# Turning attention probabilities with 64-row transposes inside the score bursts of a two-layer encoder

## The chip, the cores and the metric

The kernel runs on one NeuronCore of one Trainium2 chip. The metric is the device time of one execution in microseconds (us), the median of several runs; lower is better. Engines are named as in the profile: PE is TensorE's matmul side, PEld its weight loads, DVE is VectorE, ACT is ScalarE, POOL is GpSimd, SP is SyncE, on whose queue the DMAs are issued.

## The reference

256 tokens of width 1024 go through two layers in float32. Layer 0 (even) has two groups of eight heads side by side: neighbourhood attention with a bias table, and latent attention (MLA). Layer 1 (odd) has 16 heads of 64; each head is a mixture of three dilated windows. Every layer ends with a squared-ReLU MLP.

```python
def odd_mixer(xn, w_in, w_o, cos_f, sin_f):
    hcat = (xn @ w_in).reshape(b, s, DIL_GROUPS, 3, DIL_HEADS, HEAD_DIM)
    q = apply_rope(hcat[:, :, :, 0], cos_f, sin_f)
    k = apply_rope(hcat[:, :, :, 1], cos_f, sin_f)
    v = hcat[:, :, :, 2]
    return dilated_attention(q, k, v) @ w_o
...
for layer in range(DEPTH):
    xn = rms_norm(x, norm_mix[layer])
    x = x + (even_mixer(...) if layer % 2 == 0 else odd_mixer(...))
    x = x + sq_relu_mlp(rms_norm(x, norm_mlp[layer]), mlp_w1[layer], mlp_w2[layer])
return rms_norm(x, norm_final)
```

Every attention is scores = q k, a softmax over the keys, and a sum of the values weighted by the probabilities.

## The kernel before

**Matrix products.** Weights stream from HBM through `load_weight` (DMA into `raw`, SP's queue) and are split by `split` into a high part (ACT, line 176) and a low part (DVE, line 177). `mm3` (lines 180 to 182) and `mm2` (lines 186 and 187) are the large products on PE in 128x128 mode; they are called "gemm" here. A gemm matmul streams 256, 384 or 512 columns.

**Attention on PE.** Three other shapes of the array occur. `two_heads` (line 201) makes the scores of two heads at once: each head has 64 rows of the array, three passes a head. The two smaller window groups of the odd layer (line 880) use 64x64 tiles. The sums of values, `mix` (lines 730, 913, 918), have 64 columns a head. Between scores and sums the probabilities must be turned so that the keys lie on partitions: `turn_probs` (even, line 714) and `turn` (odd, line 898) do this with transposes of 128x128 blocks on PE, in the shape of the gemm, and a copy out of PSUM (lines 716, 900).

**PSUM** has eight banks, four under the tag "w" and four under "acc". `bank(tag)` takes them in turn, and an instruction that writes a bank waits until the readers of its last use are done.

**Even layer.** `attention()` gives a list of 35 side steps that is spread over the gemm steps of `main` by a cost per step. `items` numbers the 16 (kind, query tile, head pair): numbers 0 to 7 are neighbourhood attention, with two query tiles t for each of the four head pairs hp, and 8 to 15 are MLA. `scores(n)` stands at side step 2n+1 (number 0 at step 0), `turn_probs(n-1)` right behind it, and the sums at n = 5 (pairs 0 and 1), 9 (2 and 3), 13, 15 and 17. A bias tile of 256 KB per item comes by DMA into one of two buffers (`load_bias`, line 679); the next load into a buffer waits for the reduction on DVE (line 699) that reads it. After it come the exponentials and the scaling on ACT (lines 704 and 707).

**Odd layer.** The 16 heads are eight units of two heads. Of each unit u, twelve gemm steps make q and k (`qk_steps`, with a swap by DMA for the rotation) and four the values. `weave` spreads the attention of unit u-1 over these 16 steps: a burst (scores by `two_heads`, then line 880, then `mix` of unit u-2) behind the first step, then four single turns with a gemm step or two between them. `mix` of unit 6 stands at the end of unit 7's gemm, the attention of unit 7 and its `mix` in the output product (`out_steps`).

The instruction order on each engine is that of a list scheduler which starts from the program's order and may put a ready instruction ahead of one that its model takes for late.

## Time and profile before

| what | us |
|---|---|
| median of 3 runs (lowest to highest) | 744.56 (744.52 to 745.54) |
| the profiled execution | 744.40 |
| its span, first to last instruction | 742.6 |
| PE busy in the span | 734.6 |
| PEld busy | 645.2 |
| DVE busy | 536.2 |
| ACT busy | 464.2 |

The granted clock of TensorE was 0.999 of full speed. The even attention lies at about 40 to 107 us of the span, the odd layer at about 305 to 562 us. Matmuls are pipelined: a matmul's row shows its latency, so what PE spends on a piece is read from the distance between starts, not from the busy time.

### The profile page before, as it was taken

To read this page: it belongs to the slowest core of one execution; us is meant where nothing else is said; L and a number is where in the kernel's file an instruction comes from. 1 tells how busy PE (TensorE), PEld (TensorE's weight loads), DVE (VectorE), ACT (ScalarE), POOL (GpSimd) and SP (SyncE) were. 2 spreads that over 40 slices of the span, in tenths; PEclk is the share of its full clock that TensorE was granted. 3 is DMA by queue.
4 is the path that set the end of the run, shared out by engine and by line. 5 is a ranking of instruction groups with operands and counts; after the bars stand their busy time and mean duration, and the time that the engine had idled before them with its cause. 6 is when DMAs were issued, how large, how long until landed. Compare 5 with 4: busy or idle time off the path is not lost.

```text
span 742.6 us, 12516 instructions
## 1 busy us (share of the span) xinstructions
PE 734.6 (99%) x4764; PEld 645.2 (87%) x4764; DVE 536.2 (72%) x1108; ACT 464.2 (63%) x1044; POOL 6.0 (1%) x16
## 2 busy tenths in 40 slices
PE   9999999999999999999999999999999999999996
PEld 6998998888888888989899899898998888888885
DVE  6798869666665666898777787787769665665664
ACT  6679967554554556767775866877757544554541
POOL 0100000000000000000000000000000000000000
PEclk9999999999999999999999999999999999999999
DMA  8966334555555444674655555565653545455401
GB/s 286 344 205 222 114 121 163 186 212 180 178 209 185 179 174 150 197 249 154 224 185 183 188 189 179 171 189 192 232 199 126 215 169 209 169 190 193 178 26 56
DMA packets 28107, 136.87 MB, mean 184 GB/s; under 512 B 4496, under 2 KB 7056, under 8 KB 14992
## 3 DMA queue, kind: packets, MB, share of 16 engines
q1 hardware_dynamic: 27760, 135.81, 53.4%
q8 instruction: 37, 0.61, 0.3%
q10 hardware_dynamic: 288, 0.28, 0.1%
q14 instruction: 22, 0.18, 0.1%
HBM read 127.68 MB, written 1.05 MB: 173 GB/s over the span
## 4 chain that ended last, share of the span: by engine, by line
PE 91%; ACT 3%; DMA 2%; issue 1%; DVE 1%; SPq 0%; POOLq 0%; POOL 0%; DVEq 0%; ACTq 0%
PE w L186 16%; PE acc L180 13%; PE acc L181 13%; PE acc L182 13%; PE acc L186 12%; PE w L187 8%; PE acc L187 6%; PE w L898 1%; PE acc L913 1%; PE w L201 1%; DMA raw<-in_w_v 1%; PE w L730 1%; DMA bias<-in_rpb 1%; PE w L714 1%; ACT whi L176 1%
## 5 line engine op out<-in xcount | busy, mean ns | idle before, releaser
L177 DVE TENSOR_TENSOR wlo<-raw,whi 128x512 fp32r<-128x512 f32 (+3 forms) x488 | 302.5, 664 | 63.5 <-ACT whi L176 63.0
L176 ACT CAST whi<-raw 128x512 fp32r<-128x512 f32 (+3 forms) x488 | 263.7, 602 | 82.6 <-issue 71.1
L186 PE MATMUL w<-xT,whi 128*128 128x512 f32 x512 | 179.4, 394 | 0.0
L186 PE MATMUL acc<-xT,whi 128*128 128x512 f32 x384 | 137.3, 401 | 0.0
L187 PE MATMUL w<-xT,wlo 128*128 128x256 f32 x512 | 132.8, 280 | 0.0
L186 PEld LDWEIGHTS w<-xT,whi 128*128 128x128 f32 x512 | 93.6, 187 | 18.3
L187 PEld LDWEIGHTS w<-xT,wlo 128*128 128x128 f32 x512 | 96.1, 188 | 5.5
L187 PE MATMUL acc<-xT,wlo 128*128 128x256 f32 x384 | 99.8, 280 | 0.0
L180 PE MATMUL acc<-whi,h 128*128 128x512 f32 x250 | 98.4, 393 | 0.0
L181 PE MATMUL acc<-wlo,h 128*128 128x512 f32 x250 | 97.8, 391 | 0.0
L182 PE MATMUL acc<-whi,h 128*128 128x512 f32 x250 | 97.4, 390 | 0.0
L186 PEld LDWEIGHTS acc<-xT,whi 128*128 128x128 f32 x384 | 70.0, 188 | 12.7
L193 ACT COPY up<-w 128x256 f32<-128x256 f32 x64 | 23.9, 374 | 88.4 <-PE w L186 88.4
L187 PEld LDWEIGHTS acc<-xT,wlo 128*128 128x128 f32 x384 | 72.2, 188 | 3.7
L194 DVE TENSOR_TENSOR up<-up,w 128x256 f32<-128x256 f32 x64 | 26.8, 419 | 63.0 <-ACT up L193 62.3
L180 PE MATMUL acc<-whi,xT 128*128 128x384 f32 (+2 forms) x160 | 56.6, 354 | 0.1
L181 PE MATMUL acc<-wlo,xT 128*128 128x384 f32 (+2 forms) x160 | 56.1, 351 | 0.3 <-DVE wlo L177 0.2
L182 PEld LDWEIGHTS acc<-whi,h 128*128 128x128 f32 x250 | 46.9, 188 | 10.1
L181 PEld LDWEIGHTS acc<-wlo,h 128*128 128x128 f32 x250 | 47.0, 188 | 9.8
L182 PE MATMUL acc<-whi,xT 128*128 128x384 f32 (+2 forms) x160 | 55.4, 346 | 0.0
L180 PEld LDWEIGHTS acc<-whi,h 128*128 128x128 f32 x250 | 46.9, 188 | 9.1
L181 PEld LDWEIGHTS acc<-wlo,xT 128*128 128x128 f32 x160 | 30.3, 190 | 3.0 <-DVE wlo L177 2.0
(194 smaller groups left out, 1021.3 us busy)
## 6 DMA issues: line engine op xcount, KB each, us to landing
raw<-in_w SPq DMA_DIRECT2D x64, 1024.0 KB, 4.8
raw<-in_w_oqk SPq DMA_DIRECT2D x24, 1024.0 KB, 5.1
raw<-in_w_ov SPq DMA_DIRECT2D x16, 768.0 KB, 4.5
sw<-qk SPq DMA_DIRECT2D x96, 64.0 KB, 2.2
raw<-in_w_qk SPq DMA_DIRECT2D x4, 1024.0 KB, 10.8
raw<-in_w_oe SPq DMA_DIRECT2D x4, 1024.0 KB, 7.1
raw<-in_w_oo SPq DMA_DIRECT2D x4, 1024.0 KB, 5.0
bias<-in_rpb SPq DMA_DIRECT2D x8, 256.0 KB, 5.4
```

The lines of the kernel that those rows point to most:

```text
L176: a = nc.scalar.copy(hi, src).ins
L177: return a, (eng or nc.vector).tensor_tensor(lo, src, hi.bitcast(F32), op=ALU.subtract).ins
L180: nc.tensor.matmul(o, sh, mh, start=first, stop=False)
L181: nc.tensor.matmul(o, sh, ml, start=False, stop=False)
L182: nc.tensor.matmul(o, sl, mh, start=False, stop=last)
L186: both = lambda: nc.tensor.matmul(o, sh, m.rearrange("p v n -> p (v n)"), start=first, stop=last)
L187: low = lambda: nc.tensor.matmul(o[:, 0:T], sl, m[:, 0, :], start=False, stop=False)
L193: nc.scalar.copy(dst, o[:, T:2 * T])
L194: nc.vector.tensor_tensor(dst, dst, o[:, 0:T], op=ALU.add)
L201: nc.tensor.matmul(o[j], qk[pb, 0, a, ts], qk[pb, 1, b, :], start=n == 0, stop=n == 2)
L714: nc.tensor.transpose(pt[:, b * P:(b + 1) * P], pp[:, b // 2, (b % 2) * P:(b % 2 + 1) * P], ident)
L730: nc.tensor.matmul(pvo[64 * j:64 * j + 64, o], v[:, kk, h * 64:(h + 1) * 64], pts[:, 2 * j + kk, :], start=kk == 0, stop=kk == NT - 1)
```

## The change

- **Odd layer, turns.** `turn(u, i)` now takes query tile i for both heads: per head three blocks of 128 keys, each by two transposes of 64 rows (rows 0 to 63 and 64 to 127 of the probabilities, with the matching 64x64 part of the identity). The two halves go to two PSUM banks `pt[0]` and `pt[1]`; two copies put them together in one tile `pts`. 12 transposes a turn in place of 6 in two turns.
- **Odd layer, place.** Both turns of unit u-1 stand in the burst of unit u: `mix(u-2)`, `turn(u-1, 0)`, the `two_heads` scores, `turn(u-1, 1)`, line 880's scores. So the sum of values of a unit comes one burst later, and the value tiles have three buffers. The turns' banks are of the tag "acc" there. The burst stands behind the second gemm step (for unit 0 behind the fourth); the burst of unit 7 stands behind step 13 of unit 7's own gemm. In the output product `last_turn` (`mix` of unit 6, both turns of unit 7) stands behind step 6 and `mix` of unit 7 behind step 9.
- **Even layer.** The two query tiles of a head pair in neighbourhood attention are one burst: `pair_scores(hp)`, 12 matmuls, at side steps 0, 5, 9 and 13. `turn_pair(hp-1)` (16 transposes of 64 rows) stands ahead of it, and ahead of that `mix(hp-2)`. The last pair (items 6 and 7) and MLA keep `turn_probs`. `mix` takes the sums of turned pairs in halves of 64 queries. `load_bias` is called behind the softmax that frees the buffer.

```diff
@@ -679,22 +679,28 @@
                 nc.sync.dma_start(biases[n], a["rpb"][t, hp])
 
         def scores(n):
-            kind, t, hp = items[n]
-            load_bias(n + 2)
-
-            sb = [bank("w")[:, 0:T] for _ in range(2)] if kind == 0 else bank("w").rearrange("p (j n) -> p j n", j=2)
-            s_of = lambda j: sb[j] if kind == 0 else sb[:, j]
-            if kind == 0:
-                two_heads(sb, qk[hp], tok(t))
-            else:
-                for j in range(2):
-                    h = 2 * hp + j
-                    q, k = (halves(mT[n][:, h]) for n in "qk")
-                    mm3(sb[:, j], q[0][:, tok(t)], q[1][:, tok(t)], *k, True, True)
+            hp = items[n][2]
+            o = bank("w").rearrange("p (j n) -> p j n", j=2)
+            for j in range(2):
+                h = 2 * hp + j
+                q, k = (halves(mT[c][:, h]) for c in "qk")
+                mm3(o[:, j], q[0][:, tok(items[n][1])], q[1][:, tok(items[n][1])], *k, True, True)
+            softmax(n, [o[:, 0], o[:, 1]])
+
+        def pair_scores(hp):
+            o = [bank("w") for _ in range(2)]
+            for t in range(NT):
+                two_heads([z[:, t * T:(t + 1) * T] for z in o], qk[hp], tok(t))
+            for t in range(NT):
+                softmax(2 * hp + t, [z[:, t * T:(t + 1) * T] for z in o])
+                load_bias(2 * hp + t + 2)
+
+        def softmax(n, s):
+            kind = items[n][0]
...
+                o = s[j]
...
             pt = bank("w")
             for b in range(4):
                 nc.tensor.transpose(pt[:, b * P:(b + 1) * P], pp[:, b // 2, (b % 2) * P:(b % 2 + 1) * P], ident)
-            turned[n] = scratch([4, P], "pts")
-            nc.any.tensor_copy(out=turned[n], in_=pt.rearrange("p (b n) -> p b n", b=4))
+            pts = scratch([4, P], "pts")
+            nc.any.tensor_copy(out=pts, in_=pt.rearrange("p (b n) -> p b n", b=4))
+            turned[n] = [(slice(0, P), lambda b: pts[:, b, :])]
+
+        def turn_pair(hp):
+
+            pt, pts = [bank("w") for _ in range(2)], [scratch([8, 64], "pts") for _ in range(2)]
+            for t in range(NT):
+                pp = probs.pop(2 * hp + t)
+                for b in range(4):
+                    for r in range(2):
+                        rows, at = slice(64 * r, 64 * r + 64), slice((4 * t + b) * 64, (4 * t + b) * 64 + 64)
+                        nc.tensor.transpose(pt[r][:, at], pp[rows, b // 2, (b % 2) * P:(b % 2 + 1) * P], ident[rows, rows])
+                turned[2 * hp + t] = [(slice(64 * r, 64 * r + 64), lambda b, t=t, r=r: pts[r][:, 4 * t + b, :]) for r in range(2)]
+            for r in range(2):
+                nc.any.tensor_copy(out=pts[r], in_=pt[r].rearrange("p (b n) -> p b n", b=8))
 
         def mix(*pairs):
             kind, _, hp = items[2 * pairs[0]]
@@ -723,29 +743,39 @@
             pvo = bank("acc" if pairs[0] < 2 else "w")
             for i, m in enumerate(pairs):
                 for t in range(NT):
-                    pts, o = turned.pop(2 * m + t), slice(i * T + t * P, i * T + t * P + P)
-                    for kk in range(NT):
-                        for j in range(2):
-                            h = 2 * (hp + i) + j
-                            nc.tensor.matmul(pvo[64 * j:64 * j + 64, o], v[:, kk, h * 64:(h + 1) * 64], pts[:, 2 * j + kk, :],
-                                             start=kk == 0, stop=kk == NT - 1)
+                    pts, o = turned.pop(2 * m + t), i * T + t * P
+                    for own, block in pts:
+                        for kk in range(NT):
+                            for j in range(2):
+                                h = 2 * (hp + i) + j
+                                nc.tensor.matmul(pvo[64 * j:64 * j + 64, o + own.start:o + own.stop], v[:, kk, h * 64:(h + 1) * 64],
+                                                 block(2 * j + kk), start=kk == 0, stop=kk == NT - 1)
             n = len(pairs)
             split(*halves(mixed[kind][:, hp:hp + n]), pvo[:, 0:n * T].rearrange("p (i n) -> p i n", i=n))
 
         def attention():
 
-            out, last = [], len(items) + 1
-            groups = {5: (0, 1), 9: (2, 3), 13: (4, 5), 15: (6,), 17: (7,)}
-            for n in range(last + 1):
+            def burst(hp):
+                if hp > 1:
+                    mix(hp - 2)
+                if hp > 0:
+                    turn_pair(hp - 1)
+                pair_scores(hp)
+
+            wait = lambda: None
+            out, last = [wait] * 17, len(items) + 1
+            for hp, n in enumerate((0, 5, 9, 13)):
+                out[n] = lambda hp=hp: burst(hp)
+            out[16] = lambda: turn_probs(6)
+            groups = {9: (2, 3), 13: (4, 5), 15: (6,), 17: (7,)}
+            for n in range(8, last + 1):
                 first = [lambda n=n: mix(*groups[n])] if n in groups else []
                 if n < len(items):
                     first.append(lambda n=n: scores(n))
                 if first:
                     out.append(lambda f=first: run_all(f))
-                if 0 <= n - 1 < len(items):
+                if n - 1 < len(items):
                     out.append(lambda n=n: turn_probs(n - 1))
-                if n == 0:
-                    out += [lambda: None] * 2
             return out
 
         ug, kg = query_steps(), key_value_steps()
@@ -795,7 +825,7 @@
             d = {}
             for n, shape, dt in (("q0", [P, 2, 2, T], F32R), ("q12", [P, 2, T], F32), ("k12", [P, 2, T], F32),
                                  ("v0", [P, NT, P], F32), ("v12", [P, 4, P], F32)):
-                d[n] = op.tile(shape, dt, tag=n, name=n, bufs=2)
+                d[n] = op.tile(shape, dt, tag=n, name=n, bufs=3 if n[0] == "v" else 2)
             return d
 
         def value_steps(d):
...
-        turned = {}
-
-        def attention(u, d, other, pause=2):
-
-
-            probs = {}
-
-            def scores():
-                ss = {(i, j): bank("w") for i in range(NT) for j in range(2)}
-                for i in range(NT):
-                    two_heads([ss[i, j][:, 0:T] for j in range(2)], d["q0"], tok(i))
-                for i in range(NT):
-                    for g in range(2):
-                        for c in range(2):
-                            for j in range(2):
-                                pb, own = slice(64 * j, 64 * j + 64), slice(i * P + 64 * c, i * P + 64 * c + 64)
-                                nc.tensor.matmul(ss[i, j][64 * c:64 * c + 64, T + 64 * g:T + 64 * g + 64], d["q12"][pb, g, own],
-                                                 d["k12"][pb, g, own], start=True, stop=True)
-                other()
-                for i in range(NT):
-                    for j in range(2):
-                        sn, pp = scratch([384], "sn"), scratch([384], "pp")
-                        mn, z, rz = (work.tile([P, 1], F32, tag=v, name=v, bufs=4) for v in ("dmn", "dz", "drz"))
-                        nc.vector.tensor_tensor_reduce(out=sn, in0=ss[i, j][:, 0:384], in1=mask[:, i, :], op0=ALU.add, op1=ALU.min,
-                                                       scale=-(HD ** -0.5), scalar=3e38, accum_out=mn)
-                        nc.scalar.activation(pp, sn, AF.Exp, bias=mn, scale=-1.0, accum_out=z)
-                        nc.vector.reciprocal(rz, z)
-                        nc.scalar.activation(pp, pp, AF.Copy, scale=rz)
-                        probs[i, j] = pp
-
-            def turn(i, j):
-                pp = probs.pop((i, j))
-                pt = bank("w")
+        probs, turned = {}, {}
+
+        def scores(u, d, between):
+
+            ss = {(i, j): bank("w") for i in range(NT) for j in range(2)}
+            for i in range(NT):
+                two_heads([ss[i, j][:, 0:T] for j in range(2)], d["q0"], tok(i))
+            between()
+            for i in range(NT):
+                for g in range(2):
+                    for c in range(2):
+                        for j in range(2):
+                            pb, own = slice(64 * j, 64 * j + 64), slice(i * P + 64 * c, i * P + 64 * c + 64)
+                            nc.tensor.matmul(ss[i, j][64 * c:64 * c + 64, T + 64 * g:T + 64 * g + 64], d["q12"][pb, g, own],
+                                             d["k12"][pb, g, own], start=True, stop=True)
+            for i in range(NT):
+                for j in range(2):
+                    sn, pp = scratch([384], "sn"), op.tile([P, 384], F32, tag="pp", name="pp", bufs=4)
+                    mn, z, rz = (work.tile([P, 1], F32, tag=v, name=v, bufs=4) for v in ("dmn", "dz", "drz"))
+                    nc.vector.tensor_tensor_reduce(out=sn, in0=ss[i, j][:, 0:384], in1=mask[:, i, :], op0=ALU.add, op1=ALU.min,
+                                                   scale=-(HD ** -0.5), scalar=3e38, accum_out=mn)
+                    nc.scalar.activation(pp, sn, AF.Exp, bias=mn, scale=-1.0, accum_out=z)
+                    nc.vector.reciprocal(rz, z)
+                    nc.scalar.activation(pp, pp, AF.Copy, scale=rz)
+                    probs[u, i, j] = pp
+
+        def turn(u, i, tag):
+
+            pt = [bank(tag) for _ in range(2)]
+            for j in range(2):
+                pp = probs.pop((u, i, j))
                 for b in range(3):
-                    nc.tensor.transpose(pt[:, b * P:(b + 1) * P], pp[:, b * P:(b + 1) * P], ident)
-                pts = turned[u, i, j] = op.tile([P, 3, P], F32, tag="pts", name="pts", bufs=6)
-                nc.any.tensor_copy(out=pts, in_=pt[:, 0:384].rearrange("p (b n) -> p b n", b=3))
-
-            wait = lambda: None
-            return [scores] + [wait] * pause + [f for i in range(NT) for j in range(2) for f in (lambda i=i, j=j: turn(i, j), wait)]
+                    at = slice((3 * j + b) * 64, (3 * j + b) * 64 + 64)
+                    for r in range(2):
+                        rows = slice(64 * r, 64 * r + 64)
+                        nc.tensor.transpose(pt[r][:, at], pp[rows, b * P:(b + 1) * P], ident[rows, rows])
+            pts = turned[u, i] = op.tile([P, 6, P], F32, tag="pts", name="pts", bufs=2)
+            for r in range(2):
+                nc.any.tensor_copy(out=pts[:, :, 64 * r:64 * r + 64], in_=pt[r][:, 0:384].rearrange("p (b n) -> p b n", b=6))
 
         def mix(u, d, out_tag):
             pvo = bank(out_tag)
             for i in range(NT):
-                pts = [turned.pop((u, i, j)) for j in range(2)]
+                pts = turned.pop((u, i))
                 at = i * P
                 for kk in range(NT):
                     for j in range(2):
                         cs = slice(64 * j, 64 * j + 64)
-                        nc.tensor.matmul(pvo[cs, tok(i)], d["v0"][:, kk, cs], pts[j][:, kk, :], start=kk == 0, stop=False)
+                        nc.tensor.matmul(pvo[cs, tok(i)], d["v0"][:, kk, cs], pts[:, 3 * j + kk, :], start=kk == 0, stop=False)
                 for c in range(2):
                     qs = slice(64 * c, 64 * c + 64)
                     for j in range(2):
                         cs = slice(64 * j, 64 * j + 64)
-                        nc.tensor.matmul(pvo[cs, at + 64 * c:at + 64 * c + 64], d["v12"][:, 2 * i + c, cs], pts[j][:, 2, qs],
+                        nc.tensor.matmul(pvo[cs, at + 64 * c:at + 64 * c + 64], d["v12"][:, 2 * i + c, cs], pts[:, 3 * j + 2, qs],
                                          start=False, stop=c == 1)
             split(*halves(mixed[u // 4][:, u % 4]), pvo[:, 0:T])
 
-        d, nd = unit_tiles(0), unit_tiles(1)
+        units = [unit_tiles(0)]
+        d = units[0]
...
+        def beside(main, placed):
+
+            for i, step in enumerate(main):
+                step()
+                if i in placed:
+                    placed[i]()
+
+        def burst(u):
+
+            def step():
+                if u > 1:
+                    mix(u - 2, units[u - 2], "acc")
+                if u > 0:
+                    turn(u - 1, 0, "acc")
+                scores(u, units[u], lambda: turn(u - 1, 1, "acc") if u > 0 else None)
+            return step
+
+        for u in range(1, 8):
+            units.append(unit_tiles(u))
+            placed = {3 if u == 1 else 1: burst(u - 1)}
+            if u == 7:
+                placed[13] = burst(7)
+            beside(qk_steps(units[u]) + all_values(units[u]), placed)
         accs, wo = open_accs(), {}
-        side = attention(7, nd, lambda: None) + [lambda: mix(7, nd, "w")]
-        weave([f for k in range(6) for f in out_steps(accs, mixed, wo, k)], side)
+
+        def last_turn():
+            mix(6, units[6], "w")
+            for i in range(NT):
+                turn(7, i, "w")
+
+        beside([f for k in range(6) for f in out_steps(accs, mixed, wo, k)], {6: last_turn, 9: lambda: mix(7, units[7], "w")})
         return accs, out_last(accs, mixed, wo)
 
     def phase(name, fn, *args):
```

More of the change, by code (lines that the diff above doesn't have):

```diff
@@ L933, in odd @@
         run_all(first[2:])
-        weave(qk_steps(nd) + all_values(nd), attention(0, d, lambda: None, 3), 3)
-        for u in range(2, 8):
-            pd, d, nd = d, nd, unit_tiles(u)
-            side = attention(u - 1, d, lambda: mix(u - 2, pd, "acc"))
-            weave(qk_steps(nd) + all_values(nd), side + [lambda: mix(6, d, "acc")] if u == 7 else side)
-        accs, wo = open_accs(), {}
-        side = attention(7, nd, lambda: None) + [lambda: mix(7, nd, "w")]
-        weave([f for k in range(6) for f in out_steps(accs, mixed, wo, k)], side)
+        def beside(main, placed):
[17 more added lines that the diff above has]
+            beside(qk_steps(units[u]) + all_values(units[u]), placed)
+        accs, wo = open_accs(), {}
+        def last_turn():
[3 more added lines that the diff above has]
+        beside([f for k in range(6) for f in out_steps(accs, mixed, wo, k)], {6: last_turn, 9: lambda: mix(7, units[7], "w")})
         return accs, out_last(accs, mixed, wo)
```

1 line of the change is left out of this document (removed).

## The prediction

> **What bounds the kernel now.** I read the profile's first part, then who waited for whom, then busy time by stretch (columns: stretch; its length; busy us and instructions of PE, PEld, DVE, ACT, POOL; clock; DMA share; GB/s).
>
> ```profile
> PE 734.6 (99%) x4764; PEld 645.2 (87%) x4764; DVE 536.2 (72%) x1108; ACT 464.2 (63%) x1044; POOL 6.0 (1%) x16
> ...
> PE w L880 <- DVE k L856: 0.2, 1, 0.2
> PE w L714 <- ACT pp L707: 0.2, 1, 0.2
> ...
> 40.00:56.00 16.00, 16.00 (x137) 14.56 (x135) 15.09 (x42) 12.41 (x36) 0.00 (x0) 1.00 0.82 241
> 56.00:82.00 26.00, 25.80 (x234) 23.23 (x235) 23.39 (x60) 24.86 (x64) 0.00 (x0) 1.00 0.53 171
> 350.00:380.00 30.00, 30.00 (x240) 27.30 (x238) 24.66 (x54) 22.24 (x55) 0.00 (x0) 1.00 0.55 185
> ```
>
> PE is the bound in both attention stages: it waits once for the others in each, 0.2 us. So time that the change takes from PE's instruction stream comes off the end, as long as the other engines keep up. In the odd stage they have room (DVE 24.66 and ACT 22.24 of 30 us). In the even stage they have little: DVE 15.09 of 16 us, then ACT 24.86 of 26 us.
>
> **Odd layer: the transposes.** First the group of all 96 turns' transposes (count; busy; mean ns), then one turn in the order of time (start, latency, engine, line, count). A matmul's cost is the distance to the next start.
>
> ```profile
> L898 PE MATMUL w<-ident,pp 128*128 128x128 f32 x96 | 15.7, 272 | 0.1
> ...
> 387.62 0.28 PE L187 MATMUL acc<-xT,wlo 128*128 128x256 f32 x1
> ...
> 387.97 0.28 PE L187 MATMUL acc<-xT,wlo 128*128 128x256 f32 x1
> ...
> 388.09 0.49 PE L898 MATMUL w<-ident,pp 128*128 128x128 f32 x3
> 388.33 0.48 PE L186 MATMUL acc<-xT,whi 128*128 128x512 f32 x1
> 388.65 0.28 PE L187 MATMUL acc<-xT,wlo 128*128 128x256 f32 x1
> ```
>
> An undisturbed L187-L186 pair takes 0.35 (387.62 to 387.97), the pair with the turn in it 0.68 (387.97 to 388.65). A turn of three transposes costs 0.33, 0.11 each, in the gemm's shape and so with no further price. 96/3 = 32 turns cost 32 x 0.33 = 10.5 us: this is removed.
>
> What a half transpose costs no row of before shows. It streams 64 columns of the identity in place of 128, and the two row halves can run side by side if the array lets them. The nearest rows are those of a burst, where PE works in 64-row or 64-column tiles:
>
> ```profile
> 408.92 0.28 PE L187 MATMUL acc<-xT,wlo 128*128 128x256 f32 x1
> 409.13 0.98 PE L201 MATMUL w<-q 64*128 64x256 f32 x12
> 410.04 0.69 PE L880 MATMUL w<-k,q 64*64 64x64 f32 x32
> 410.67 0.66 PE L913 MATMUL acc<-pts,v 128*64 128x128 f32 x8
> 411.15 0.40 PE L918 MATMUL acc<-pts,v 128*64 128x64 f32 x8
> 411.38 0.61 PE L913 MATMUL acc<-pts,v 128*64 128x128 f32 x8
> ...
> 382.36 0.50 PE L186 MATMUL acc<-xT,whi 128*128 128x512 f32 x1
> 382.70 0.28 PE L187 MATMUL acc<-xT,wlo 128*128 128x256 f32 x1
> ```
>
> L918: eight float32 passes of 64 columns, two at a time, take 0.23 (411.15 to 411.38): 0.058 a pair. L201: twelve passes of 64 rows take 0.91. In the gemm a 256-column pass takes 0.12 (387.97 to 388.09); twelve in a row would be 1.4, so two 64-row tiles do run side by side. I take 0.058 a pair of half transposes: the lower end. The upper end is 0.058 for each half, 0.116 a pair, nothing side by side. I stand at the lower because L201 has the very shape (64 rows, 128 columns) and L918 the width.
>
> The Trainium skill ("TensorE: Matmul & The Clock Gate", What overlaps and what doesn't) says that a weight load overlaps a running matmul only when their row groups differ. By that a pair would pay load and pass one after the other, near the upper end, and the forecast would be that of the first rival below. L201's 0.91 for six pairs of loads and passes speaks against it.
>
> A turn is 6 pairs: 6 x 0.058 = 0.35; 16 turns: 5.6 us. Changes of shape: the switch into L201 costs 0.21 - 0.12 = 0.09 at its start, that out of the burst 382.36 to 382.70, 0.34 where 0.35 - 0.12 = 0.23 is usual, 0.11. Before, a burst passes through four shapes and back (gemm, L201, L880, mix, gemm); after, gemm, mix, turn and L201 in one shape, L880, gemm: as many. For the first load of each of the eight turn groups that no pass hides I add 0.1: 0.8. The lone `mix` of unit 6 had two switches, with both turns of unit 7 behind it three: +0.15. There the fifth "w" bank is that of `mix` itself and waits for its split: one wait of some 0.3. Between 0 and 1 us would be the ends.
> Odd sum: -10.5 + 5.6 + 0.8 + 0.15 + 0.3 = -3.65.
>
> Moved at no cost: the copies of turned blocks (four a unit before and after) and the softmax, on DVE and ACT with the room above; the sum a unit later has its value tiles buffered three times. Its price if that cover goes is the second rival. Unit 7's burst moves ahead into its own gemm, where two value steps in place of five gemm steps lie between the last product of k and line 880; PE's one wait there (0.2, in the first fence) bounds what I count at nothing, and the scheduler has two value steps more to put in between.
>
> **Even layer.** Single steps as they stand among gemm passes:
>
> ```profile
> 48.46 0.28 PE L182 MATMUL acc<-xT,wlo 128*128 128x256 f32 x1
> 48.67 0.62 PE L201 MATMUL w<-qk 64*128 64x256 f32 x6
> 49.22 0.39 PE L180 MATMUL acc<-xT,whi 128*128 128x256 f32 x1
> 49.44 0.28 PE L181 MATMUL acc<-xT,whi 128*128 128x256 f32 x1
> ...
> 50.64 0.28 PE L182 MATMUL acc<-xT,wlo 128*128 128x256 f32 x1
> 50.76 0.60 PE L714 MATMUL w<-ident,pp 128*128 128x128 f32 x4
> 51.11 0.36 PE L180 MATMUL acc<-xT,whi 128*128 128x256 f32 x1
> 51.31 0.28 PE L181 MATMUL acc<-xT,whi 128*128 128x256 f32 x1
> ...
> 58.68 1.53 PE L730 MATMUL acc<-pts,vna 128*64 128x128 f32 x24
> 60.14 0.38 PE L201 MATMUL w<-qk 64*128 64x256 f32 x1
> 60.45 0.66 PE L730 MATMUL acc<-pts,vna 128*64 128x128 f32 x8
> 61.04 0.62 PE L201 MATMUL w<-qk 64*128 64x256 f32 x5
> 61.59 0.39 PE L180 MATMUL acc<-c,whi 128*128 128x256 f32 x1
> ```
>
> - Scores: a burst of six takes 48.46 to 49.44 = 0.98, less two gemm passes of 0.12: 0.74. Twelve take 0.91 - 0.55 = 0.36 more. Each merged pair saves 0.74 - 0.36 = 0.38; four: -1.5.
> - Turns: four transposes take 50.64 to 51.31 = 0.67 - 0.24 = 0.43. Six turns go (-2.6); three `turn_pair` of eight pairs come, 8 x 0.058 + 0.06 for the first load = 0.52, +1.6. Net -1.0.
> - Sums: those of pairs 0 and 1 take 58.68 to 61.59 = 2.91, with the six scores in between and a score pass (0.31) that split them; with 0.2 of switches 3.1, less 0.74 for the scores 2.4. After: two `mix` of 16 passes' pairs at 0.058 = 0.93 and one switch of 0.15 each, 2.2. Pair 2 in halves +0.06. Net -0.1.
>
> Sum on PE: -2.6. How much of it the stage gives is open, since DVE and ACT are nearly full and bias tiles come later relative to their use:
>
> ```profile
> 50.18 0.33 SPq L679 DMA_DIRECT2D bias<-in_rpb  x1
> ...
> 56.28 0.42 DVE L699 CUSTOM_DVE_ANT_0 sn<-w,bias 128x256 f32<-128x256 f32 x1 [0.81 <-DMA bias<-in_rpb]
> ```
>
> Bias 4 is issued at 50.18 and DVE waits 0.81 for it until 56.28. After, bias 5 is wanted in the same burst, two side steps (about 3 us) earlier than now, issued right behind bias 4 on SP's queue; the weight loads stand behind both. DVE's queue is in order, so its reduction holds the weight splits behind it. Against that, the softmax of the second tile now starts two steps earlier, where ACT has 3.6 us free (12.41 of 16), and probabilities are wanted four steps after their scores. Ends: all of the 2.6, or none and up to 2 us of waits more. I take 1.0 of waits: -1.6.
>
> **The sum.** 744.40 - 3.65 - 1.6 = 739.15 us for an execution like the profiled one, which lies 0.16 under the median of 744.56. I forecast 739.2; own range 737.0 to 740.8 (even gain whole and the odd layer's 0.8 + 0.15 + 0.3 nearly at nothing; even gain nil).
>
> **Rivals.**
>
> *The halves do not pay.* Each half runs alone, 0.70 a turn: odd -10.5 + 11.2 + 1.25 = +1.95, even 24 pairs x 0.058 = 1.4 dearer, -0.2: 746.1. If load and pass follow each other within the half, about 0.11 a pair: odd 16 x 0.65 = 10.4, +1.15, even -0.4: 745.2; without the even waits 744.2. For it: no such transpose in the trace. Against: L201 and L880 with two row halves at once, and their scores of the two halves go to two banks just as `pt[0]` and `pt[1]` do.
>
> The same is weighed from another side by the Trainium skill ("TensorEngine Tiling (Array Packing)", Instruction Overhead): a matmul has some 60 cycles of overhead, and no tiling factor should be taken from a dimension that is already small. By it 64 columns would be the edge of what still pays. Rows L913 and L918 show 64 columns at half the cost of 128: (411.15 - 410.67)/4 = 0.12 against 0.058 a pair.
>
> *The other side: the sum's bank holds up the burst.* In an odd burst `mix`, both turns take five "acc" banks of four: the second bank of `turn(u-1, 1)` is that of `mix(u-2)`, and PE must wait for its split.
>
> ```profile
> 384.58 0.37 ACT L176 CAST oa<-acc 128x256 fp32r<-128x256 f32 x1
> 384.98 0.42 DVE L177 TENSOR_TENSOR oa<-acc,oa 128x256 fp32r<-128x256 f32 x1 [0.23 <-ACT oa L176]
> ...
> 526.24 0.19 PEld L180 LDWEIGHTS acc<-whi,xT 128*128 128x128 f32 x1
> 526.99 0.43 DVE L177 TENSOR_TENSOR ob<-acc,ob 128x256 fp32r<-128x256 f32 x1
> ```
>
> Now a burst's `mix` ends at 382.36 and its split at 384.98 + 0.42 = 385.40, 3.0 us later, behind the softmax. In the new burst the bank is wanted after one turn and L201, 0.35 + 0.91 = 1.3 us. Were the split as late, six bursts would wait 1.7 us: +10.4, 749.6. It decides from (746.05 - 739.2)/6 = 1.1 us a burst. Against: `mix` now leads the burst, so its split stands ahead of the softmax, and where it stands alone (unit 6, gemm again at 526.24) the split ends at 527.42, 1.2 us. A small wait of 0.2 a burst is in my own range.
>
> *The even gain turns into waits, or turns fall out of their burst.* With 2 us of waits more than the even gain, 739.15 + 1.6 + 2 = 742.8; or seven second turns are put among gemm passes because their bank is taken for late, two switches of 0.1 to 0.15 each, +1.4 to 2.1: 741. For it: DVE's and ACT's fill, and the split sum at 60.14, an order that the kernel's text does not have. 740.8 to 743.
>
> **How the numbers follow.** Mine 0.55; even waits or fallen turns 0.27; halves that do not pay 0.10; the bank 0.08. About 0.2% (1.5 us, 743.05 to 746.05) is what a measurement of this kernel can tell from no change. Faster: 0.55 + 0.27 = 0.82. Same: nearly all of the halves' case, 0.08. Slower: the bank and the rest, 0.10. The range leaves out the last two cases, 0.18: 736.8 to 743.2, the lower end with the even gain whole and the odd layer's 1.25 at nothing (736.9).
>
> **What would show it.** L898's successor in the changed profile: 192 transposes of 64*128, two starts together, a turn of twelve in 0.35 to 0.45; if they start one by one, the halves do not pay. The distance from one odd burst to the next down by 0.45 to 0.5. PE waits at the turns' line behind DVE or ACT `oa`/`ob`: the bank. Scores in 12s in the even layer and PE waits behind DVE or ACT between 50 and 80 us: the even gain given back. The prediction is wrong above all if the halves run singly or if DVE's queue stalls on a bias tile.

## The result and the profile after

| | before | after |
|---|---|---|
| median us (lowest to highest, 6 runs each) | 744.79 (744.52 to 745.54) | 749.01 (747.78 to 750.15) |
| the profiled execution, us | 744.40 | 749.12 |
| its span | 742.6 | 747.3 |
| PE busy | 734.6 | 731.1 |

The ratio of the medians is 1.0055, 95% interval 1.0045 to 1.0065: the changed kernel is slower by 0.55%. 739.2 was forecast. PE is busy for 3.5 us less, as the change meant, and yet the span is 4.7 us longer: time went from work into waits. The first part of the profile after:

```profile
PE 731.1 (98%) x4932; PEld 641.7 (86%) x4932; DVE 537.2 (72%) x1111; ACT 464.2 (62%) x1043; POOL 6.0 (1%) x16
```

The waits of PE after (what waited for what: us in total, times, the longest):

```profile
PE acc L929 <- DVE oa L177: 3.0, 4, 0.7
PE acc L180 <- ACT vml L666: 1.9, 1, 1.9
...
PE acc L929 <- ACT pts L932: 1.1, 1, 1.1
PE acc L929 <- DVE ob L177: 0.7, 1, 0.7
```

In the changed kernel, line 929 is the odd layer's half transposes, 932 their copies, 942 and 947 its sums, 907 its 64x64 scores (line 880 before); 733 is the even half transposes and 751 the even sums. Line 929 waits for the split of `oa` and `ob`, the output of `mix`: a wait that the kernel before does not have. The stretches that answer to those shown of before (stretch; length; busy us and instructions of PE, PEld, DVE, ACT, POOL; clock; DMA share; GB/s):

```profile
350.00:380.00 30.00, 28.86 (x230) 26.13 (x231) 22.83 (x51) 21.80 (x53) 0.00 (x0) 1.00 0.57 185
...
40.00:56.00 16.00, 16.00 (x178) 15.24 (x179) 14.65 (x42) 14.30 (x40) 0.00 (x0) 1.00 0.75 239
56.00:82.00 26.00, 24.06 (x272) 22.09 (x273) 22.74 (x59) 24.22 (x61) 0.00 (x0) 1.00 0.58 184
```

Before, PE stood still in these stretches for 0.20 us in all, in the second of the even ones; now it does for 1.14 of 30 us in the odd layer and 1.94 of 26 in the even one. The 1.14 is the wait behind `pts`, in the burst of unit 1; the first burst with a `mix` in it comes at 379.

**An odd burst, by its rows.** PE's timeline after (start, latency, line, count, and in brackets the idle time before and what ended it):

```profile
379.28 0.66 PE L942 MATMUL acc<-pts,v 128*64 128x128 f32 x8
379.76 0.40 PE L947 MATMUL acc<-pts,v 128*64 128x64 f32 x8
...
380.43 0.40 PE L947 MATMUL acc<-pts,v 128*64 128x64 f32 x8
380.76 0.58 PE L929 MATMUL acc<-ident,pp 64*128 64x64 f32 x12
381.16 0.96 PE L201 MATMUL w<-q 64*128 64x256 f32 x12
381.96 0.21 PE L929 MATMUL acc<-ident,pp 64*128 64x64 f32 x1
382.91 0.59 PE L929 MATMUL acc<-ident,pp 64*128 64x64 f32 x11 [0.74 <-DVE oa L177]
383.43 0.69 PE L907 MATMUL w<-k,q 64*64 64x64 f32 x32
384.05 0.50 PE L186 MATMUL acc<-xT,whi 128*128 128x512 f32 x1
...
413.75 0.46 PE L907 MATMUL w<-k,q 64*64 64x64 f32 x16
```

The first turn takes 381.16 - 380.76 = 0.40. If the second took as long, it would lose 1.07 us, since it takes 383.43 - 381.96 = 1.47. Its first half transpose runs; the second one, 0.95 later, is the first that writes the second bank. From burst to burst it is 413.75 - 383.43 = 30.32, against 410.04 - 380.25 = 29.79 before; without the loss it would be 29.25. The burst of before that starts this distance:

```profile
380.25 0.69 PE L880 MATMUL w<-k,q 64*64 64x64 f32 x32
```

DVE and ACT in the changed kernel, in the stretch of the burst, an answer for each:

```profile
380.89 0.42 DVE L194 TENSOR_TENSOR qk<-qk,acc 128x256 f32<-128x256 f32 x1 [0.58 <-ACT qk L193]
381.23 1.29 DVE L177 TENSOR_TENSOR wlo<-raw,whi 128x512 fp32r<-128x512 f32 x2
382.44 0.42 DVE L177 TENSOR_TENSOR oa<-acc,oa 128x256 fp32r<-128x256 f32 x1
```

```profile
380.76 0.63 ACT L176 CAST whi<-raw 128x512 fp32r<-128x512 f32 x1
381.28 0.38 ACT L176 CAST oa<-acc 128x256 fp32r<-128x256 f32 x1
```

`mix` leaves PE at 380.76. Its split is two steps, one on each engine: ACT's stands behind a weight cast, DVE's behind a step of the rotation and two weight splits of 0.65 each. So the bank comes free at 382.44 + 0.42 = 382.86, 2.10 us behind `mix` and 0.90 behind the time at which the second turn starts. Over a whole unit neither engine is full (22.83 and 21.80 of 30 us above), and the wait is there all the same: what counts is what stands ahead of one instruction in its engine's queue.

### The profile page after: what moved, and what is told of

Same layout as the page of the kernel before. It is cut to its first block, busy times and chain, and to the rows that moved or that the text cites. A ratio compares the mean times of both kernels' runs of the same rounds, so it can differ in the third digit from the quotient of the medians.

```text
span 747.3 us, 12828 instructions
## 1 busy us (share of the span) xinstructions
PE 731.1 (98%) x4932; PEld 641.7 (86%) x4932; DVE 537.2 (72%) x1111; ACT 464.2 (62%) x1043; POOL 6.0 (1%) x16
## 4 chain that ended last, share of the span: by engine, by line
PE 85%; ACT 7%; DVE 3%; DMA 2%; issue 1%; SPq 0%; POOLq 0%; POOL 0%; DVEq 0%
PE w L186 16%; PE acc L180 13%; PE acc L181 13%; PE acc L182 13%; PE acc L186 10%; PE w L187 8%; PE acc L187 5%; ACT whi L176 3%; DVE wlo L177 1%; DMA raw<-in_w_v 1%; PE w L751 1%; DMA bias<-in_rpb 1%; ACT v L851 1%; ACT v L852 1%; PE w L907 1%
## 5 line engine op out<-in xcount | busy, mean ns | idle before, releaser
L186 PE MATMUL acc<-xT,whi 128*128 128x512 f32 x384 | 134.6, 397 | 0.0
L193 ACT COPY qk<-acc 128x256 f32<-128x256 f32 x48 | 17.6, 367 | 31.8 <-PE acc L186 31.6
```

The costliest lines, as they stand in the source:

```text
L186: both = lambda: nc.tensor.matmul(o, sh, m.rearrange("p v n -> p (v n)"), start=first, stop=last)
L193: nc.scalar.copy(dst, o[:, T:2 * T])
```

## The experiments

The theory: the second turn of a burst writes the PSUM bank of `mix`, and PE waits for its split. Rivals: the half transposes cost more than they save; the even layer or the number of changes of shape makes the loss; the wait only moves when its bank is taken away. Ratios are to the kernel before on the same chip, with 95% intervals.

**Which layer.** `odd_only` has the odd layer of after and the even layer of before, `even_only` the other way round:

```diff
# odd_only: only the hunks of the odd layer
+                d[n] = op.tile(shape, dt, tag=n, name=n, bufs=3 if n[0] == "v" else 2)
+        def scores(u, d, between):
+        def turn(u, i, tag):
+        def burst(u):
# even_only: only the hunks of attention() in the even layer
+        def pair_scores(hp):
+        def turn_pair(hp):
+            def burst(hp):
```

> Odd layer as changed, even layer as before. Theory A (the loss is the wait of the second turn in each odd burst for a PSUM bank): the changed kernel's odd layer is 4.5 us longer than before in its trace (six bursts with a wait of about 1.07, one of 1.35, the last group 0.7 more, less 0.5 a unit that the half transposes save), so 744.8 + 4.5 = 749.3 (748.3 to 750.3). Theory B (the start of the kernel, 1.0 us later in the changed profile, is the price of the change and not chance, for instance through the loading of a larger program): about 750.3, with the first gain transposes of the span again 1.0 us later. Theory C (even and odd hinder each other by shared buffers): well under 748.

> Even layer as changed, odd layer as before. Theory A: the changed trace has the even attention 0.7 us shorter, with one wait of PE of 1.9 to 2.4 for an 'acc' bank behind the copy of the MLA values: 744.8 - 0.7 = 744.1 (743.3 to 744.9), the same wait in the trace. Theory B (the late start belongs to the change): 745.1.

Measured: `odd_only` 750.12, ratio 1.0066 (1.0049 to 1.0082); `even_only` 744.82, 1.0003 (0.9992 to 1.0014). The whole loss is the odd layer's. The even layer's change is worth nothing that shows in the time, though its PE work shrank. In the one profile of `even_only` the even stage is shorter, 65.02 us against 66.18 before from the first score product to the last sum, with a wait of 1.6 behind `vml` in it; but its first column sum comes 1.25 us later than in the profile of before.

**The bank, by order.** `sum_second` lets one turn pass ahead of `mix`, so that `mix` no longer holds the bank that the second turn takes. The price is one more change of shape in each burst.

```diff
-            pts = turned[u, i] = op.tile([P, 6, P], F32, tag="pts", name="pts", bufs=2)
+            pts = turned[u, i] = op.tile([P, 6, P], F32, tag="pts", name="pts", bufs=4)
...
-                if u > 1:
-                    mix(u - 2, units[u - 2], "acc")
                 if u > 0:
                     turn(u - 1, 0, "acc")
+                if u > 1:
+                    mix(u - 2, units[u - 2], "acc")
```

> The changed kernel, but in each odd burst the first turn stands ahead of mix, so that the second turn's second bank is the first turn's and no longer that of mix (pts gets four buffers for it). Theory A: the wait of about 1.07 in each of the six bursts with a mix goes, one more change of shape (0.15) comes: 749.0 - 6 x 0.92 = 743.5 (742.8 to 745.0); the bursts are 30.33 - 0.92 = 29.4 us apart. Rival (DVE and ACT are simply late in the burst, whatever bank it is): the wait moves to another bank or to the gemm behind the burst and the bursts stay 30.2 to 30.4 apart, 748.5 to 749.5.

`sum_last` puts `mix` at the end of the burst instead, behind line 907, and has the four `pts` buffers of `sum_second` too:

```diff
-        def scores(u, d, between):
+        def scores(u, d, between, behind=lambda: None):
...
+            behind()
...
-                if u > 1:
-                    mix(u - 2, units[u - 2], "acc")
-                scores(u, units[u], lambda: turn(u - 1, 1, "acc") if u > 0 else None)
+                scores(u, units[u], lambda: turn(u - 1, 1, "acc") if u > 0 else None,
+                       lambda: mix(u - 2, units[u - 2], "acc") if u > 1 else None)
```

> The changed kernel, but mix stands at the end of each odd burst, as before the change (pts gets four buffers). The second turn's second bank is then the first turn's or that of the gemm step ahead of the burst, and it is wanted 0.4 + 0.8 = 1.2 us after the burst's start, where the first turn's copies and the gemm's reading end about 2.0 us after it in the changed trace. Theory A: a wait of about 0.8 stays, about 0.3 less a burst: 749.0 - 1.6 = 747.4 (745.5 to 748.5). Rival (the wait is that of the sum's split alone, other banks are free in time): all of 1.07 goes, 742.6.

Measured: `sum_second` 745.69, 1.0007 (0.9996 to 1.0018); `sum_last` 750.06, 1.0067 (1.0052 to 1.0082). PE's timeline of `sum_second`:

```profile
379.72 0.59 PE L929 MATMUL acc<-ident,pp 64*128 64x64 f32 x12
380.33 0.66 PE L942 MATMUL acc<-pts,v 128*64 128x128 f32 x8
...
381.82 0.98 PE L201 MATMUL w<-q 64*128 64x256 f32 x12
382.63 0.54 PE L929 MATMUL acc<-ident,pp 64*128 64x64 f32 x12
383.10 0.69 PE L907 MATMUL w<-k,q 64*64 64x64 f32 x32
...
412.65 0.69 PE L907 MATMUL w<-k,q 64*64 64x64 f32 x32
```

The second turn takes 383.10 - 382.63 = 0.47, and a burst comes every 412.65 - 383.10 = 29.55 us, 0.77 less than after. So the wait for the bank is the cause of the longer bursts, and the rival of engines that are late whatever the bank (bursts 30.2 to 30.4 apart) falls. Since the same turn takes 0.47 here without a wait, the 1.07 above may count 0.07 too much, and the period without the loss may be 29.32. The time itself missed what was expected, 743.5 and at most 745.0: the odd stage is 4.2 us shorter than after (268.54 against 272.71), but a wait of 1.2 stayed in the burst of unit 1, and in this profile the even stage, whose text is the same, is 1.3 longer (66.73 against 65.45). PE's waits in `sum_last`:

```profile
PE acc L930 <- DVE qk L194: 3.5, 5, 0.7
PE acc L180 <- ACT vml L666: 1.9, 1, 1.9
```

The wait for `oa` is gone there too, but the second turn (line 930 there) now takes the bank of the gemm step ahead of the burst, whose rotation on DVE reads it late: 3.5 us in all, about as long as the wait that was removed (3.0 and 0.7). One such burst, DVE's row first, then PE's:

```profile
383.16 0.42 DVE L194 TENSOR_TENSOR qk<-qk,acc 128x256 f32<-128x256 f32 x1 [0.59 <-ACT qk L193]
```

```profile
382.74 0.21 PE L930 MATMUL acc<-ident,pp 64*128 64x64 f32 x1
383.63 0.58 PE L930 MATMUL acc<-ident,pp 64*128 64x64 f32 x11 [0.69 <-DVE qk L194]
```

The rotation's step ends at 383.58 and PE goes on at 383.63. So the theory holds in a wider form than I had it: two turns take four "acc" banks in 1.6 us, and in both orders without work between them a bank was wanted before the queues of DVE and ACT had let it go. Of the orders tried, the one that puts 1.5 us of PE work (`mix`) between the turns is without that wait; the four `pts` buffers, which `sum_last` has too, are not what helped. `sum_last` stayed far above the 747.4 that I expected: its odd stage is only 0.63 shorter than after (272.08), and in its profile the even stage is 2.45 longer (67.90), with the same text.

**The price of the half transposes.** `full_turns` is `sum_second` with transposes of all 128 rows, `halves_apart` is `sum_second` with the transposes of the upper rows ahead of all those of the lower:

```diff
# full_turns
+                    nc.tensor.transpose(pt[j][:, b * P:(b + 1) * P], pp[:, b * P:(b + 1) * P], ident)
# halves_apart
+            for r in range(2):
+                rows = slice(64 * r, 64 * r + 64)
+                for j in range(2):
+                    for b in range(3):
```

> The kernel with the first turn ahead of mix (sum_second), but the odd layer's turns are transposes of 128 rows again, in the same places, six a turn. It prices the half transposes by themselves. Theory (a pair of halves goes side by side at about 0.06, a whole one at 0.108): a turn 0.65 in place of 0.36, the same number of changes of shape, 16 turns: 745.7 + 4.6 = 750.3, the bursts 29.55 + 0.6 = 30.1 apart. Rival (the halves save nothing, the changed kernel's odd layer suffers from them): 745 to 746, bursts 29.5 apart.

> The kernel with the first turn ahead of mix (sum_second), but each odd turn issues its six transposes of the upper rows first and then its six of the lower rows, so that neighbours on PE have the same rows. Theory (only neighbours of different rows run side by side): 12 x 0.058 = 0.70 a turn in place of 0.36, 16 x 0.34 = 5.4 more: about 751, bursts 30.2 apart. Rival (PE finds the overlap by itself among queued instructions, or a half costs 0.03 anyway): unchanged, 745.7, bursts 29.55 apart.

Measured: `full_turns` 748.31, 1.0042 (1.0026 to 1.0058); `halves_apart` 748.16, 1.0030 (1.0011 to 1.0049, with times from 745.68 to 748.73). Bursts of `full_turns`:

```profile
382.04 0.98 PE L201 MATMUL w<-q 64*128 64x256 f32 x12
382.95 0.88 PE L926 MATMUL acc<-ident,pp 128*128 128x128 f32 x6
383.75 0.69 PE L907 MATMUL w<-k,q 64*64 64x64 f32 x32
...
413.78 0.40 PE L907 MATMUL w<-k,q 64*64 64x64 f32 x12
```

The turn takes 0.80 against 0.47, and the period is 30.03 against 29.55: 0.24 for each of its two turns is what the halves save. They do pay, so the rival falls, but for less than the 750.3 that was expected: 748.31 is 2.6 above `sum_second`. Its odd stage is 2.74 longer (271.28 against 268.54), a little less than 0.24 for each of 16 turns, among other things because the wait in unit 1 is 0.5 there and not 1.2. In `halves_apart` the turn takes 0.65:

```profile
383.96 0.71 PE L929 MATMUL acc<-ident,pp 64*128 64x64 f32 x12
384.61 0.58 PE L907 MATMUL w<-k,q 64*64 64x64 f32 x24
...
414.43 0.69 PE L907 MATMUL w<-k,q 64*64 64x64 f32 x32
```

and the period is 29.82, 0.27 longer, where 0.65 would have been two turns of halves one by one. The time lies between the two that were expected (751 and 745.7). The single records show why: the first three start 0.056 to 0.061 apart, and then others begin 2 to 7 ns beside them, so that part of the halves still goes in pairs. Whether that is the order the scheduler made or the engine's own doing, the records don't tell.

**The other waits.** `even_sums_w` is `even_only` with the sums of pairs 0 and 1 in a "w" bank, because the longest even wait is for an "acc" bank. `no_waits` is `sum_second` with that edit too, and with the second turn of unit 0 behind line 907 and one of the last two turns ahead of the last-but-one `mix`:

```diff
# even_sums_w and no_waits
-            pvo = bank("acc" if pairs[0] < 2 else "w")
+            pvo = bank("w")
# no_waits
-                scores(u, units[u], lambda: turn(u - 1, 1, "acc") if u > 0 else None)
+                second = lambda: turn(u - 1, 1, "acc")
+                scores(u, units[u], second if u > 1 else lambda: None, second if u == 1 else lambda: None)
...
+            turn(7, 0, "w")
             mix(6, units[6], "w")
-            for i in range(NT):
-                turn(7, i, "w")
+            turn(7, 1, "w")
```

> Even layer as changed, odd layer as before (even_only), but the sums of head pairs 0 and 1 go to banks of the tag w instead of acc, so that the MLA products find an acc bank. Theory A (the 1.6 to 2.1 us of waiting near 66 us is for acc banks that the sums occupy while their split is queued): the wait goes, 744.8 - 1.7 = 743.1; at 107 us the stage is 1.5 to 2 earlier relative to its first scores. Rival (ACT and DVE are full there, so whatever PE saves comes back as another wait): the waits' sum in the even stage stays at 1.5 or more and the time at 744.3 to 745.3.

> sum_second with the other bank waits of the changed kernel taken away as well: the second turn of unit 0 behind line 907's scores (1.35 in the burst of unit 1), in the output product the order turn, mix, turn (0.77), and the even sums in w banks (1.8). Theory A: 745.7 - 1.2 - 0.5 - 1.7 = 742.3 (741.3 to 743.5), faster than before by 0.2 to 0.5%. Rival (each wait taken away comes back elsewhere): 744.5 to 746.

Measured: `even_sums_w` 744.58, 0.9998 (0.9989 to 1.0008); `no_waits` 743.80, 0.9982 (0.9972 to 0.9991). PE's waits of `even_sums_w`:

```profile
PE acc L180 <- ACT whi L176: 1.3, 1, 1.3
...
PE w L201 <- ACT pts L736: 1.0, 1, 1.0
```

The wait for `vml` is gone and two others have come: one for a split weight, one for a "w" bank whose turned block ACT copies late. That is what the rival expected, 744.3 to 745.3, and not 743.1. `no_waits` has no wait above 0.4 but the one at the kernel's start that all of them have:

```profile
PE acc L90 <- DVE warm L84: 1.2, 1, 1.2
PE acc L180 <- ACT v L852: 0.4, 1, 0.4
...
PE acc L930 <- ACT pts L933: 0.4, 1, 0.4
PE w L201 <- ACT pts L736: 0.4, 1, 0.4
```

It beats both kernels, by 0.18% of the one before. 742.3 was expected, with 743.5 as the upper end, so only a part of the waits' worth came. No other version that was measured is clearly better; two below can't be told from it.

**Bias tiles, and the odd layer alone.** The softmax of the even layer had waited for bias tiles, from 0.2 us in the profile of `even_only` to 1.6 in that of `sum_last`. `even_bias3` is `even_only` with three bias buffers and the load three items ahead (one scratch buffer fewer makes the room), `no_waits_bias3` adds the same to `no_waits`, and `odd_no_waits` is the odd layer of `no_waits` with the even layer of before:

```diff
# even_bias3 and no_waits_bias3
-        v = work.tile([P, 512], F32, tag="scratch", name=name, bufs=12)[:, :n]
+        v = work.tile([P, 512], F32, tag="scratch", name=name, bufs=11)[:, :n]
...
-                biases[n] = ep.tile([P, 2, T], F32, tag="bias", name="bias", bufs=2)
+                biases[n] = ep.tile([P, 2, T], F32, tag="bias", name="bias", bufs=3)
...
-                load_bias(2 * hp + t + 2)
+                load_bias(2 * hp + t + 3)
# odd_no_waits: the hunks of attention() in the even layer are left out of no_waits
```

> Even layer as changed, odd layer as before (even_only), with three bias buffers in place of two, so that a bias tile is loaded three items ahead and not two (the shared scratch tile has 11 buffers for it, not 12). Theory (part of the even loss is DVE's queue held up by a bias transfer, 0.2 to 1.6 us in the profiles so far): the waits of the bias reduction behind the bias DMA go, the even attention takes 64.5 to 65.5 us from its first scores to its last sum, 744.8 - 1.0 = 743.8. Rival (ACT is full from 56 to 82 us and sets the pace whatever DVE waits for): the wait of 1.6 to 2.2 us of PE behind the copy of the MLA values stays and the time is 744.5 to 745.0.

> no_waits with the same three bias buffers. Theory: 743.8 - 0.5 to 1.0 = 743.0. Rival (ACT sets the even pace): 743.8, unchanged within 0.5.

> Even layer as before the change, odd layer as in no_waits (first turn ahead of mix, unit 0's second turn behind line 907, turn-mix-turn in the output product). It tells which layer gives no_waits its 0.2%. By the stages of the profiles (odd 267.3 against 268.2 before, even 65.7 against 66.2): 744.9 - 0.95 = 743.9 if the odd layer alone gives it; 744.9 if the even layer does.

Measured: `even_bias3` 743.85, 0.9988 (0.9978 to 0.9998); `no_waits_bias3` 744.03, 0.9986 (0.9977 to 0.9996); `odd_no_waits` 744.76, 1.0001 (0.9991 to 1.0010). In the profile of `even_bias3` the wait for `vml` stands at 1.6 as in that of `even_only`, and the even stage is as long (64.99 against 65.02 us from the first score product to the last sum), so its 0.1% can't be put down to the bias tiles, though 743.8 was the very time that the theory expected. The two profiles differ by 0.95 us, and the start makes that difference: the first column sum comes at 19.50 against 20.50. Beside the other changes the bias tiles bring nothing. `odd_no_waits` has two waits that `no_waits` lacks or has smaller, behind the copies of values and the rotated keys:

```profile
PE acc L913 <- ACT v L822: 0.6, 1, 0.6
PE w L877 <- DVE k L856: 0.6, 2, 0.4
```

They are the 1.0 us by which its odd layer is longer (268.30 against 267.26 us from the last `diagonal` product to the final MLP's column sums; before 268.21, after 272.71). The text of the odd layer is the same in both, so waits of that size come and go with what stands elsewhere, and they are as large as what is left to gain. By its time, near the 744.9 expected if the even layer gives the gain, `odd_no_waits` would put the 0.18% of `no_waits` down to the even layer; with those waits in its odd stage, the question stays open.

## Why the prediction was wrong

- **The step that failed** is the weighing of the second rival, "the sum's bank holds up the burst", with a chance of 0.08. The odd sum of -3.65 has no term for it. The rival named the place and the bank rightly. Its price of 1.7 us a burst was too high: 1.07 was measured, just under the 1.1 at which it was said to decide alone, and the waits below made up the rest. What was wrong was the reason against it, "its split stands ahead of the softmax, and where it stands alone ... the split ends at 527.42, 1.2 us". The softmax was not what had to be passed. In a burst the split stands behind the weight splits and the rotation that serve the gemm on both sides, and took 2.10 us; the bank was wanted after 1.20. The row of a lone split was taken for one that stands in the thick of the gemm's own stream. The measured 2.10 lies midway between the two rows of before, 1.2 alone and 3.0 beside a burst; the forecast was built on the lower one.
- **The room of DVE and ACT.** "In the odd stage they have room" was right as an average (22.83 and 21.80 of 30 us after) and proves nothing about the delay of one instruction.
- **"Moved at no cost": the copies of turned blocks.** In unit 1, where there is no `mix`, PE waited for the first turn's copies on ACT (the 1.1 behind `pts` in the waits after): the first copy begins at 352.05 and takes 0.48, and PE goes on 0.05 later. That turn took 353.10 - 351.23 = 1.87 in place of 0.40, so 1.5 was lost. Two turns alone fill the four banks just once, so why the second turn had to wait for that copy the trace does not show.

```profile
351.23 0.21 PE L929 MATMUL acc<-ident,pp 64*128 64x64 f32 x1
352.58 0.58 PE L929 MATMUL acc<-ident,pp 64*128 64x64 f32 x11 [1.14 <-ACT pts L932]
```

- **The fifth "w" bank at the last turns, 0.3.** Twelve pairs of halves should take some 0.75; from 545.04 to 546.56 they took 1.52, so the term was 0.8, inside the ends of 0 and 1 that were given.
- **Even waits, 1.0 us.** The even work came as forecast: scores in twelves, `turn_pair` in 0.52 or 0.53 (48.87 to 49.40), exactly the estimate, `mix` in 1.08.

```profile
48.87 0.71 PE L733 MATMUL w<-ident,pp 64*128 64x64 f32 x16
49.40 0.95 PE L201 MATMUL w<-qk 64*128 64x256 f32 x12
54.79 1.15 PE L751 MATMUL acc<-pts,vna 128*64 128x64 f32 x32
55.87 0.71 PE L733 MATMUL w<-ident,pp 64*128 64x64 f32 x16
...
66.34 0.39 PE L182 MATMUL acc<-whi,c 128*128 128x512 f32 x1
68.66 0.39 PE L180 MATMUL acc<-c,whi 128*128 128x256 f32 x1 [1.94 <-ACT vml L666]
```

  But one wait of 2.1 us at 66.34, for an "acc" bank that ACT copies out late, takes back most of the 2.6. The even stage is 0.73 shorter in the profile after (65.45 against 66.18 us), 1.6 was forecast, and by the medians of `even_only` nothing is left. The prediction took 1.0 for waits and looked for them above all at DVE and its bias tiles; the one that came was at ACT, for a bank again.
- **What was right.** The half transposes: pairs start 0.058 to 0.060 apart, the two of a pair 3 ns apart; a turn takes 0.39 to 0.40 where 0.35 was taken, and 16 x 0.04 = 0.7 of the 0.8 set aside for first loads is just that. The rival of halves that do not pay fell. The period without the wait, 29.25 to 29.32, is 0.47 to 0.54 below that of before; 0.45 to 0.5 was forecast. PE's busy time fell by 3.5. All of the work side of the sum was sound; the waits were not.

The odd layer by its parts: five bursts x 1.07 = 5.4 (5.0 by the 0.47 of `sum_second`), 1.5 in unit 1, 0.4 in unit 7's burst and 0.5 more than forecast at the last turns are 7.8 us of waits, where the forecast of -3.65 and the measured 272.71 - 268.21 = +4.50 differ by 8.15. With the even stage's -0.73 that makes +3.77 of the 4.7 us between the two profiles. The rest is 1.0 us at the kernel's start, where both kernels issue the same instructions: over the thirteen profiles of this case the first column sum came at 19.25 to 20.51 us, with the same order of instructions up to it. The profile of before is the earliest of them.

Why the repaired version gains 1.2 and not 5: the order that has no wait pays one more change of shape, and so a period of 29.55 in place of 29.25 to 29.32; the even gain did not come; and small waits move about. The order with the shorter period and no wait was not reached.

What stays open: how much of the even layer's PE gain could be had, since each wait that was taken away there was followed by another; and why even stages of the same program text lay between 65.0 and 67.9 us from profile to profile (waits for bias tiles of 0.2 to 1.6 us are a part of that).

## What to carry to other kernels

Before work is packed into a burst, count the PSUM banks that the burst takes and compare the time to the second use of each with the time of its readers, measured at a place where their queues are as they will be there, with everything queued ahead. An engine's free share says nothing on that. If a bank is short, put other PE work between its two uses; taking another bank, or an order that puts no work between, may only move the wait, as `sum_last` and `even_sums_w` showed here.

## What the runs showed of the hardware

- Two half transposes on different rows of the array start 3 ns apart; two on the same rows start 0.055 to 0.065 us apart, although each brings a weight load of its own whose record lasts 0.138. The plainest rows for that are in `halves_apart`, in the second turn of unit 1: the six lower halves wait for their bank there, so the six upper ones run by themselves, and then the lower ones do (the first step behind the wait is 0.111). The Trainium skill ("TensorE: Matmul & The Clock Gate", What overlaps and what doesn't) lets a load overlap only when the row groups differ. By that, load and pass would follow each other in `halves_apart`; its records show no such pause.
- The Trainium skill ("TensorEngine Tiling (Array Packing)", Gotcha 1: PSUM Pressure) says that row tiles write to different PSUM banks and so put pressure on PSUM. In this case a turn does write its halves to two banks, and a burst with two turns and a sum takes five out of four; PE paid some 1.0 us a burst for the fifth. But the whole transposes of `full_turns` take two banks a turn as well, so the price is that of the burst and not of the row tiles alone.
- A change of shape inside a burst has a price that the difference of the two orders shows: 29.55 us a period against the 29.25 to 29.32 worked out for the other order without its wait: an estimate of 0.2 to 0.3 us for a turn that stands apart from the scores of its own shape.
